# Softmax attention with keys on partitions in two mixers of a four-layer network

## The chip, the cores and the metric

The program runs on one core of one Trainium2 chip, as one launch. Its time is device microseconds for that core. Five engines work side by side, each through an instruction queue of its own: TensorE (PE) multiplies, VectorE (DVE), ScalarE (ACT) and GpSimd (POOL) do elementwise work, SyncE (SP) starts DMAs. Matrix products land in PSUM, everything else is in SBUF.

## The reference

One sequence of 512 tokens with 1024 features passes two blocks. The first has two layers of forgetting attention and sparse attention. The second, where the change lies, has an even layer and an odd layer, each a mixer followed by layer norm, an expert layer and another layer norm. The two attentions in question attend in both directions, in fp32:

```python
# even layer: MLA, 8 heads, 64 + 32 features for the scores (32 rotary key features shared by all heads)
s = (jnp.einsum('bqhd,bkhd->bhqk', qn, k_nope) + jnp.einsum('bqhd,bkd->bhqk', qp, k_pe)) * scale
pr = jax.nn.softmax(s.astype(jnp.float32), axis=-1).astype(v.dtype)
return jnp.einsum('bhqk,bkhd->bqhd', pr, v)
...
# odd layer: 16 query heads of 64 in 4 groups that share keys and values, RMS norm and rotary on q and k
sc = jnp.einsum('bqkgd,bskd->bkgqs', qb, k) * scale
pr = jax.nn.softmax(sc.astype(jnp.float32), axis=-1).astype(v.dtype)
return jnp.einsum('bkgqs,bskd->bqkgd', pr, v)
```

## The kernel before

All activations stay in SBUF with features on partitions and the 512 tokens along the free axis. A product in full precision is made of fp32r passes over exact high and low parts (`h`, `l`): weight parts `whi`, `wlo` by activation parts, three passes for each 128x128 tile of weights (`mm3`). The split of the weights is a cast on ACT and a subtraction on DVE or POOL (L220). Products written as fp32 without a split (`o`, `ss`, `rt`) are recorded as two passes each.

Both mixers handle heads in pairs: four pairs in MLA (`even_mixer`, L1029), eight in the odd mixer (L1703). For one pair `full_pair` (L988) puts 128 queries on partitions. For each half of the queries and each head it makes two score tiles `s` with all 512 keys along the free axis (L1001: three passes in MLA, two in the odd mixer); DVE finds each row's maximum (L1002); ACT takes the exponential with the maximum as bias and adds up the row (L1003); DVE scales the rows by the reciprocal of the sum (L1004, L280). The probabilities are then transposed on PE in 128x128 tiles (`pt`, L1015, sixteen for each half and head), copied to SBUF by DVE (L1021) or ACT (L1019), and multiplied with the values: L1026 writes 64 partitions of `o` for each head, 256 queries at a time, over four tiles of keys. `put_split` (L492) leaves the parts of `o` for the output projection: a cast on ACT (L493) and a subtraction on DVE (L494).

In MLA a pair's queries `qn` and keys `kn` are projected in the loop and scaled into the tiles Q and K, which hold 64 own features and 32 rotary ones of each head; the rest of the query tile is zeroed once by POOL memsets (L1123). In the odd mixer `normed_rope` projects the 128 features of a pair (`qk`), takes their mean squares (`ss`), ACT forms the reciprocal root (L262, L263), the rotation goes through PE (`rt`, L1740) and the two halves of the rotary product are made by DVE (L1742) and POOL (L1743). Keys of a half of the groups come first and again at the fourth pair. The value projection `tm` (L520 to L522) follows the first query projection.

Two pieces of other work fall into the odd mixer's start. The layer norm before it hands over the activations tile by tile: ACT copies the transposed tile, DVE makes its parts (cast L1396, subtraction L1397). POOL multiplies the token-major copy `xtok` by a gain and adds a bias (L1789, L1790), four tiles of 128x1024 each.

The order on each engine is not that of the text. A scheduler moves instructions at build time by its own timing of the dependences, with the order of the text as its start; the pools of tiles (`bufs`) bound how far work can run ahead. The queues then run in that order.

Of the kernel before, what the change touches and what calls it, by code (L numbers as in the profile page):

```python
# [10 lines left out]
F32 = mybir.dt.float32  # L11
# [20 lines left out]
def constants():  # L32
# [10 lines left out]
    # partial rotary: the first 16 of 64 features, pairs (i, i + 8)  # L43
# [21 lines left out]
    # axial rotary  # L65
# [22 lines left out]
    c["before"] = before  # L88
    c["slot"] = np.tile(np.arange(64, dtype=f32)[None, :], (128, 1))
# [3 lines left out]
def layout(inputs):  # L93
    """The arrays as the device takes them: values moved, none computed."""
# [10 lines left out]
    # blocks of 512 rows and columns, and of 256 columns, by partition  # L105
# [20 lines left out]
class Parts(list):  # L126
    """hi and lo of 1024 features, a tile for each 128; a tile can serve as float32 scratch before."""
# [17 lines left out]
class K:  # L145
# [5 lines left out]
    def open(self, es):  # L151
# [10 lines left out]
        # gains of the first block's norms: mix 0, mix 1, mlp 0, mlp 1, final  # L162
# [42 lines left out]
    def split(self, view, pool=False):  # L205
        """Exact two-part split of fp32 weights [128, k, ...]: hi + lo, each float32r [128, k, n]."""
# [16 lines left out]
    def mm3(self, ps, wh, wl, xh, xl, first=True, last=True):  # L223
        """One k-tile of a product, weights stationary: wh*xh + wh*xl + wl*xh."""
# [5 lines left out]
    def proj(self, ps, view, xh, xl, first=True, last=True, pool=False):  # L230
        """ps[m, t] += sum_k view[k, m] x[k, t] over view's k-tiles."""
# [5 lines left out]
    def exp_ln_table(self):  # L237
        """One table of ScalarE that serves Exp and Ln alike."""
# [6 lines left out]
    def add_square(self, pool, ss, x, m):  # L245
        """Sum of squares over eight feature tiles, one at a time."""
# [12 lines left out]
    def rstd_of(self, pool, ss, n, out):  # L259
        """out = (ss / n + eps) ** -0.5"""  # L260
# [11 lines left out]
    def rowvec(self, pool, src, n, name):  # L272
        """[128 * n] of DRAM to [128, n], feature k*128 + p at [p, k]."""
# [64 lines left out]
    def block1(self, xT, A, B):  # L338
        """Both layers of the first block; the final norm's input parts are left in A."""
# [21 lines left out]
    def mixer1(self, l, A, B, mp, mixed, xT, cp):  # L361
        """The two attentions' outputs, hi/lo, into B from the normed input's parts in A."""
# [3 lines left out]
        with ExitStack() as es:  # L366
# [11 lines left out]
            # rstd by token  # L378
# [43 lines left out]
            # running sums of log sigmoid, in two float32r parts: rows 0-7 hi, rows 32-39 lo  # L422
# [20 lines left out]
    def fox(self, l, at, pp, w, XH, XL, v, cneg, B, comp):  # L443
# [19 lines left out]
        def attend(pr):  # L463
# [32 lines left out]
    def log1p_exp_neg(self, p, a, name):  # L496
        """log(1 + exp(-a)) for a >= 0, exact where exp(-a) is small."""
# [11 lines left out]
    def token_major(self, pp, src, XH, XL, outs, rT, tag="mm"):  # L509
        """outs[t][tok, 256] = rstd * (x @ src) with tokens on partitions."""  # L510
# [16 lines left out]
    def token_wide(self, pp, src, XH, XL, outs, rT, first):  # L527
        """outs[t][tok, 512] = rstd * (x @ src) with tokens on partitions."""
# [20 lines left out]
    def rope_in(self, at, rc, rs, z):  # L549
        """z <- z * C + swap(z) * S, the swap within groups of 32 partitions."""  # L550
# [9 lines left out]
    def q_stack(self, at, pp, wv, XH, XL, rope):  # L560
        """Two heads' queries, scaled by 1/8, as [hi; lo] (first) and [lo; hi] (second)."""
# [22 lines left out]
    def causal_scores(self, at, pp, Q, KH, qh, kl, extra=None):  # L584
        """exp(s - max) of a head, four query tiles; and their sums [128, 4]."""
# [22 lines left out]
    def causal_pv(self, at, pp, o, P, cf, V, first, last):  # L608
        """o[64h.., q] += sum_k V[h][k]^T (cf * P)^T for two heads."""
# [22 lines left out]
    def nsa(self, l, p, at, pp, w, XH, XL, gate, gcmp, B, KC, VC, fill):  # L632
# [17 lines left out]
        # vs | vw, tokens on partitions  # L650
# [14 lines left out]
        for g in range(2):  # L665
# [5 lines left out]
            # compressed branch of the four heads  # L671
# [63 lines left out]
    def compress(self, l, p, at, pp, w, XH, XL, B, mixed):  # L735
        """Compressed keys (float32r hi, lo on both halves) and values (four copies of 32 rows)."""
# [3 lines left out]
        # the first product's weights, four rows of [2, 128, 256] each  # L740
# [27 lines left out]
        for kv in range(2):  # L768
# [65 lines left out]
    def merge_fox(self, l, mp, at, pp, w, XH, XL, B, mixed, th):  # L834
        """mixed = the first branch's output by its gate, doubled."""
# [29 lines left out]
    def merge1(self, l, xs, A, B, mixed, ready):  # L865
        """mixed = sigmoid(gates) * branch outputs; x += mixed @ w_out; the mlp's input parts into B."""
# [44 lines left out]
    def new_x(self, p, ss, xs, m, g, B):  # L911
        """Feature tile m is final: its squares into ss, its scaled parts into B."""
# [6 lines left out]
    def mlp1(self, l, xs, A, B):  # L919
        """x += relu(h @ w_up) ** 2 @ w_down; the next layer's input parts into B."""  # L920
# [43 lines left out]
    # ================= block 2 =================  # L964
# [115 lines left out]
    def mla(self, XH, XL, B, pp, lr, sg, silu):  # L1080
# [3 lines left out]
        with ExitStack() as es:  # L1084
# [5 lines left out]
            with ExitStack() as e2:  # L1090
# [33 lines left out]
                for _ in range(2):  # L1124
                    next(silu)
# [686 lines left out]
```

## Time and profile before

| | |
|---|---|
| median of 3 runs | 3559.79 us (3554.05 to 3563.22) |
| profiled execution, span | 3556.4 us |
| PE busy | 3368.4 us, 95% |
| DVE, ACT, POOL busy | 1612.2, 1057.3, 499.1 us |
| share of PE in the chain that ended last | 87% |
| MLA's attention | about 1832 to 1922 us in the span |
| odd mixer with the first part of its output projection | about 2680 to 2912 us |

A row of the timeline gives start, duration and what the instruction waited for; "x8" joins eight in a row. Durations of matmuls overlap, since they are pipelined: the time from one start to the next tells what one costs. In the windows "PEclk" is the granted clock of PE, 1.00 for 2.4 GHz and 0.50 for 1.2 GHz; a value between is a mean over the stretch.

### The profile page before, as it was taken

How to read it: one execution, taken by the hardware profiler on the slowest of the kernel's cores; microseconds unless marked ns; L12 is line 12 of the kernel's file. 1: busy time of each engine (PE TensorE's matmuls, PEld its weight loads, DVE VectorE, ACT ScalarE, POOL GpSimd, SP SyncE). 2: the span in 40 equal slices, each digit the busy share in tenths (PEclk: the TensorE clock that was granted, in tenths of full speed). 3: DMA queues.
4: the chain of work that ended last, by engine and by line, in shares of the span. 5: the costliest groups of instructions: out<-in, count | busy, mean ns of one | idle time of the engine just before them, and what ended most of it. 6: DMA issues, size and time to landing. Idle time of an engine off the chain costs nothing.

```text
span 3556.4 us, 37806 instructions
## 1 busy us (share of the span) xinstructions
PE 3368.4 (95%) x15178; PEld 2159.7 (61%) x15178; DVE 1612.2 (45%) x2560; ACT 1057.3 (30%) x1897; POOL 499.1 (14%) x326
## 2 busy tenths in 40 slices
PE   8999999999999999999989879999998997999997
PEld 6666578887766657888766653444435665344443
DVE  6555464335554546344566651312226764221223
ACT  4333332223333333232364311111114541111111
POOL 2012120002001202001121430000004113000001
PEclk9999999999999999999999889999998998999999
DMA  5111132233211113332220339789881024988986
GB/s 180 48 46 50 31 101 95 95 114 115 68 51 36 48 36 100 99 98 95 66 76 13 121 131 419 322 361 381 353 349 61 24 97 197 402 344 357 384 341 273
DMA packets 219647, 584.85 MB, mean 164 GB/s; under 512 B 17232, under 2 KB 156880, under 8 KB 168272
## 3 DMA queue, kind: packets, MB, share of 16 engines
q1 hardware_dynamic: 219040, 581.66, 43.8%
q8 instruction: 119, 1.95, 0.2%
q10 hardware_dynamic: 432, 0.79, 0.1%
q14 instruction: 56, 0.46, 0.0%
HBM read 580.30 MB, written 2.10 MB: 164 GB/s over the span
## 4 chain that ended last, share of the span: by engine, by line
PE 87%; DVE 7%; ACT 2%; DMA 1%; issue 1%; POOL 0%; SPq 0%; DVEq 0%; ACTq 0%; POOLq 0%
PE a L1611 13%; PE mm L226 8%; PE mm L228 8%; PE mm L227 8%; PE y L1611 7%; PE o L629 3%; PE ga L1622 2%; PE pt L620 2%; PE o L1026 2%; PE s L597 2%; PE mg L226 1%; PE mg L228 1%; PE mg L227 1%; PE s L1001 1%; DMA w<-in_w_dram 1%; PE pt L1015 1%
## 5 line engine op out<-in xcount | busy, mean ns | idle before, releaser
L217 ACT CAST whi<-w 128x1024 fp32r<-128x1024 f32 (+1 forms) x312 | 311.3, 1003 | 740.5 <-PE mm L227 504.6
L1611 PE MATMUL a<-w,xg 128*64 128x512 f32 x2048 | 503.5, 600 | 7.5 <-DMA w<-in_w_dram 7.5
L226 PE MATMUL mm<-h,whi 128*128 128x512 f32 x1056 | 417.7, 396 | 4.9 <-ACT whi L217 4.2
L227 PE MATMUL mm<-l,whi 128*128 128x512 f32 x1056 | 414.2, 393 | 0.0
L228 PE MATMUL mm<-h,wlo 128*128 128x512 f32 x1056 | 413.7, 393 | 0.4 <-POOL wlo L220 0.3
L220 DVE TENSOR_TENSOR wlo<-w,whi 128x1024 fp32r<-128x1024 f32 (+1 forms) x240 | 308.3, 1288 | 225.1 <-ACT whi L217 224.4
L1611 PEld LDWEIGHTS a<-w,xg 128*64 128x64 f32 x2048 | 156.2, 137 | 288.0 <-issue 269.6
L220 POOL TENSOR_TENSOR wlo<-w,whi 128x1024 fp32r<-128x1024 f32 x72 | 158.6, 2205 | 832.3 <-ACT whi L217 740.7
L1611 PE MATMUL y<-w,hT 128*64 128x512 f32 x1024 | 253.7, 598 | 0.2 <-DMA w<-in_w_dram 0.2
L226 PEld LDWEIGHTS mm<-h,whi 128*128 128x128 f32 x1056 | 198.7, 188 | 50.7 <-ACT whi L217 5.4
L228 PEld LDWEIGHTS mm<-h,wlo 128*128 128x128 f32 x1056 | 198.5, 188 | 47.5 <-DVE wlo L220 1.0
L227 PEld LDWEIGHTS mm<-l,whi 128*128 128x128 f32 x1056 | 198.7, 188 | 43.5 <-issue 0.7
L601 DVE TENSOR_REDUCE mx<-s 128x1 f32<-128x128 f32 x192 | 93.3, 489 | 192.3 <-PE s L600 191.3
L1695 DVE TENSOR_TENSOR xtok<-xtok,sc 128x512 f32<-128x512 f32 x128 | 83.8, 683 | 180.6 <-PE sc L1693 180.6
L1611 PEld LDWEIGHTS y<-w,hT 128*64 128x64 f32 x1024 | 75.5, 136 | 132.9 <-issue 125.1
L603 ACT ACTIVATE P<-s,mx 128x128 f32<-128x128 f32 x192 | 100.9, 527 | 175.4 <-DVE mx L601 163.2
L947 POOL TENSOR_TENSOR u<-u 128x512 f32<-128x512 f32 x64 | 66.5, 1040 | 521.6 <-ACT E L946 275.5
L1668 POOL TENSOR_TENSOR og<-OH,aff 128x512 f32<-128x512 f32 x16 | 16.8, 1048 | 723.6 <-PE ot L1671 696.1
L958 DVE TENSOR_TENSOR y<-mm,r 128x512 f32<-128x512 f32 x64 | 44.2, 691 | 160.6 <-PE mm L228 160.6
L1660 DVE SCALAR_TENSOR_TENSOR th<-th,a 128x512 f32<-128x512 f32 x32 | 22.0, 686 | 198.5 <-ACT th L1659 198.5
L226 PE MATMUL mm<-E,whi 128*128 128x512 f32 x256 | 99.6, 389 | 0.0
L228 PE MATMUL mm<-E,wlo 128*128 128x512 f32 x256 | 99.6, 389 | 0.0
(589 smaller groups left out, 6278.3 us busy)
## 6 DMA issues: line engine op xcount, KB each, us to landing
w<-in_w_dram SPq DMA_DIRECT2D x384, 1024.0 KB, 9.9
w<-in_w_in_dram SPq DMA_DIRECT2D x32, 1024.0 KB, 5.3
w<-in_w_up_dram SPq DMA_DIRECT2D x32, 1024.0 KB, 5.4
w<-in_w_down_dram SPq DMA_DIRECT2D x32, 1024.0 KB, 5.0
w<-in_w_out_dram SPq DMA_DIRECT2D x8, 1024.0 KB, 5.0
w<-in_w_o_dram SPq DMA_DIRECT2D x8, 1024.0 KB, 4.8
w<-in_ple_gate_w_dram SPq DMA_DIRECT2D x8, 1024.0 KB, 6.4
w<-in_w_in_even_dram SPq DMA_DIRECT2D x7, 1024.0 KB, 5.5
```

Source lines behind the costliest of these rows:

```text
L217: nc.scalar.copy(h, view)
L220: e.tensor_sub(l, view, h)
L226: mm(ps, wh, xh, start=first, stop=False)
L227: mm(ps, wh, xl, start=False, stop=False)
L228: mm(ps, wl, xh, start=False, stop=last)
L597: nc.tensor.matmul(s[:, :n], qh[:, qs], kl[:, :n], start=False, stop=False)
L601: nc.vector.tensor_reduce(mx[:, i:i + 1], s[:, :n], axis=X, op=OP.max, negate=True)
L603: nc.scalar.activation(pv, s[:, :n], AF.Exp, bias=mx[:, i:i + 1], accum_out=sums[:, i:i + 1])
L620: nc.tensor.transpose(ps[:, (i - k) * 128:(i - k + 1) * 128], P[h][0][i][:, k * 128:(k + 1) * 128], C["ident"])
L629: nc.tensor.matmul(o[64 * h:64 * h + 64, 128 * k:], V[h][k], PT[h][:, :n], start=first and k == 0, stop=last and k == 3)
L1611: nc.tensor.matmul(ps[64 * a:64 * a + 64], lhs(a, 4 * kc + k), cw[a][:, k], start=kc == 0 and k == 0, stop=kc == 1 and k == 3)
L1695: nc.vector.tensor_add(xs, xs, ps)
```

## The change

`full_pair` goes. In its place the scores are made with keys on partitions, so that their exponentials need no transposing before the product with the values.

The maximum of each query's row is found from a cheaper product first (`max_steps`): for each head four single passes of the high parts alone give `s` with queries on partitions, DVE reduces each of them into one column of a tile `mt`, one transposition on PE turns the columns into rows, and DVE spreads the negated maxima over four rows of the query tile, block by block with the constant `diag4`. The key tiles hold ones in these four rows, so the score product itself subtracts the maximum (to the precision of that product, which softmax cancels).

`attend_steps` then makes the score tiles `st` (128 keys by 512 queries, L1023), takes their exponentials without bias or sums (L1025, six tiles `PT`), adds up three of four tiles for the sums (`acc`, L1030: two additions on POOL, one on DVE), multiplies them with the values, 512 queries at a time (L1036), and sums over the partitions by a product with ones (`sm`, L1041). Ln and Exp on ACT give the reciprocal, DVE multiplies, `put_split` follows.

Steps are now lists of small functions, and `weave` calls the steps of several lists by their place in the interval given to each: in MLA the pair j with the maxima of pair j+1; in the odd mixer the pair j, the maxima of j+1 and the projection of j+2, with the second keys at the second pair.

With that go: tiles with rows of zeros and ones (memsets on POOL, in MLA four for each of two key parts and their ones, in the odd mixer sixteen of 64 or 128 partitions at its start and eight small ones), a second query tile per head in the odd mixer (cast on POOL), all of its weight splits on POOL (every fourth to every one before), three PSUM buffers less one for `mm` and one more for `o`, a load of the ACT table for Exp and Ln ahead of MLA's attention, and the gain and bias of `xtok` in pieces of 512 columns, eight and eight.

```diff
+    def weave(self, *lists):
+        at = sorted((a + (b - a) * (i + 0.5) / len(s), n, i)
+                    for n, (s, a, b) in enumerate(lists) for i in range(len(s)))
+        for _, n, i in at:
+            lists[n][0][i]()
+
+    def max_steps(self, pp, q, k, mt, r0, dst):
...
+        def one(i):
+            s = pp.tile([128, T], F32, name="s", tag="s")
+            nc.tensor.matmul(s, q[:, 128 * i:128 * i + 128], k, start=True, stop=True)
+            nc.vector.tensor_reduce(mt[:, r0 + i:r0 + i + 1], s, axis=X, op=OP.max, negate=True)
+
+        def spread():
+            ps = pp.tile([128, 128], F32, name="mt", tag="mm")
+            nc.tensor.transpose(ps, mt, C["ident"])
+            rows = slice(r0, r0 + 4)
+            nc.vector.tensor_tensor(dst[rows]..., ps[rows, None, :]..., C["diag4"][rows]..., op=OP.mult)
+        return [lambda i=i: one(i) for i in range(4)] + [spread]
+
+    def attend_steps(self, at, pp, passes, V, B, j):
...
+        def score(h, k):
+            s = pp.tile([128, T], F32, name="st", tag="t")
+            for n, (kk, qq) in enumerate(passes[h]):
+                nc.tensor.matmul(s, kk[:, 128 * k:128 * k + 128], qq, start=n == 0, stop=n == len(passes[h]) - 1)
+            pt = PT[h, k] = at.tile([128, T], F32, name="PT", bufs=6)
+            nc.scalar.activation(pt, s, AF.Exp)
+            if k == 0:
+                acc[h] = at.tile([128, T], F32, name="acc")
+            else:
+                e = nc.vector if k == 3 else nc.gpsimd
+                e.tensor_add(acc[h], PT[h, 0] if k == 1 else acc[h], pt)
+
+        def values(k):
+            if k == 0:
+                o.append(pp.tile([128, T], F32, name="o", tag="o"))
+            for h in range(2):
+                nc.tensor.matmul(o[0][64 * h:64 * h + 64], V[h][k], PT[h, k], start=k == 0, stop=k == 3)
+
+        def norm():
+            sm = pp.tile([128, T], F32, name="sm", tag="o")
+            for h in range(2):
+                nc.tensor.matmul(sm[64 * h:64 * h + 64], C["ones"][:, :64], acc[h], start=True, stop=True)
+            r = at.tile([128, T], F32, name="rn", tag="PT", bufs=6)
+            nc.scalar.activation(r, sm, AF.Ln)
+            nc.scalar.activation(r, r, AF.Exp, scale=-1.0)
+            nc.vector.tensor_mul(r, r, o[0])
+            self.put_split(B, j, r)
+        sc = [lambda h=h, k=k: score(h, k) for k in range(4) for h in range(2)]
+        va = [lambda k=k: values(k) for k in range(4)]
+        return sc[:6] + va[:1] + sc[6:7] + va[1:2] + sc[7:] + va[2:] + [norm]
...
@@ even_mixer: the loop over pairs
+            tail(0)
+            for j in range(4):
+                V = ...
+                steps = self.attend_steps(at, pp, passes[j], V, B, j)
+                if j < 3:
+                    prepare(j + 1)
+                self.weave((steps, 0, 1), (tops[j + 1] if j < 3 else [], 0.1, 0.8))
...
@@ odd_mixer: keys, queries and the loop over pairs
+                for h in range(2):
+                    r0 = 64 - 64 * h
+                    nc.gpsimd.memset(kl[h][r0:r0 + 64].bitcast(F32), 0.0)
+                    nc.gpsimd.memset(kl[h][r0:r0 + 4].bitcast(F32), 1.0)
+                    nc.vector.tensor_sub(kl[h][64 * h:64 * h + 64], z[own], kh[own])
...
+                    nc.gpsimd.tensor_copy(q2[own], z[own])
+                    steps += self.max_steps(pp, q, kh, mt[j % 2][h], oth.start, q2)
+                    passes[j].append([(kh, q), (kl[h], q2)])
...
+            for j in range(8):
+                g = j // 2
+                V = [[v[:, k, 64 * g:64 * g + 64] for k in range(4)]] * 2
+                lists = [(self.attend_steps(at, pp, passes[j], V, B, j), 0, 1)]
+                if j < 7:
+                    lists.append((queries(j + 1), 0.1, 0.7))
+                if j < 6:
+                    lists.append((project(j + 2), 0.05, 0.45 if j == 1 else 0.6))
+                if j == 1:
+                    lists.append((keys(1), 0.45, 1))
+                self.weave(*lists)
+                s = slice(512 * (j % 2), 512 * (j % 2) + 512)
+                xt = self.xtok[:, j // 2, s]
+                nc.gpsimd.tensor_mul(xt, xt, G[:, s])
+                nc.gpsimd.tensor_add(xt, xt, Bb[:, s])
-                if j < 4:
-                    xt = self.xtok[:, j]
-                    nc.gpsimd.tensor_mul(xt, xt, G)
-                    nc.gpsimd.tensor_add(xt, xt, Bb)
```

In the orders below, `s` and `st` are score tiles before and after with their operands, `pt` transposed probabilities, `o` value products, `sm` sums, `ss` and `rt` the mean squares and the rotation of a projection, `qk` a projection. "x8" joins equal rows.

PE in MLA, in the midst of the second pair, before:

```order
L1001 MATMUL s<-K01h,l_2530 128x512
L1015 MATMUL pt<-c_ident,P 128x128 x8
L1001 MATMUL s<-K01h,h_2528 128x512
L1001 MATMUL s<-K01l,h_2528 128x512
L1001 MATMUL s<-K01h,l_2530 128x512
L1026 MATMUL o<-PT,vm 64x256 x3
L1015 MATMUL pt<-c_ident,P 128x128 x4
L1026 MATMUL o<-PT,vm 64x256
```

And after, at the like place (L1002 is the maximum product for the pair behind):

```order
L1023 MATMUL st<-h_2528,K01h 128x512
L1036 MATMUL o<-PT,vm 64x512
L1023 MATMUL st<-l_2529,K00h 128x512
L1023 MATMUL st<-h_2527,K00l 128x512
L1023 MATMUL st<-h_2527,K00h 128x512
L1036 MATMUL o<-PT,vm 64x512
L1002 MATMUL s<-K10h,h_3401 128x512 x2
L1023 MATMUL st<-l_2530,K01h 128x512
```

The transpositions are gone; the value products, in groups of one to four before, stand singly with three score passes between them, and the next pair's maximum products lie in the gaps.

PE in the odd mixer, in the midst of a pair before:

```order
L1026 MATMUL o<-PT,vo 64x256 x3
L1015 MATMUL pt<-c_ident,P 128x128 x4
L1026 MATMUL o<-PT,vo 64x256
L1001 MATMUL s<-kh_18437,Q_18878 128x512
L1001 MATMUL s<-kl_18438,Q_18878 128x512
L1015 MATMUL pt<-c_ident,P 128x128 x4
L227 MATMUL qk<-l_17521,whi 128x512
L228 MATMUL qk<-h_17513,wlo 128x512
```

And after, at the end of a pair, where its sums product stands:

```order
L1023 MATMUL st<-Q_17831,kh_17565 128x512
L1792 MATMUL ss<-sq,c_ones_17494 128x512
L1023 MATMUL st<-Q_17518,kl_17566 128x512
L1002 MATMUL s<-kh_17565,Q_17831 128x512
L1041 MATMUL sm<-acc,ones 64x512 x2
L1798 MATMUL rt<-z,c_rot 128x512
L1007 MATMUL mt<-c_ident,mt_17501 128x128
L1023 MATMUL st<-Q_17827,kh_17565 128x512
L1023 MATMUL st<-Q_17518,kl_17566 128x512
L1036 MATMUL o<-PT,vo 64x512
```

Where the projection of the pair and its scores alternated with transpositions, the sums product, the rotation, a transposition of maxima and the first scores of the next pair now follow each other.

POOL at the start of the odd mixer, before:

```order
L1668 TENSOR_TENSOR og<-OH,aff 128x512
L220 TENSOR_TENSOR wlo<-w,whi 128x1024
L1789 TENSOR_TENSOR xtok<-xtok,lng 128x1024 x4
L1790 TENSOR_TENSOR xtok<-xtok,lnb 128x1024 x4
L1743 TENSOR_TENSOR z<-z,c_gc 128x512 x2
L220 TENSOR_TENSOR wlo<-w,whi 128x1024 x2
```

And after:

```order
L222 TENSOR_TENSOR wlo<-w,whi 128x1024 x2
L1881 TENSOR_TENSOR xtok<-xtok,lng 128x512 x4
L1882 TENSOR_TENSOR xtok<-xtok,lnb 128x512
L1881 TENSOR_TENSOR xtok<-xtok,lng 128x512 x4
L1882 TENSOR_TENSOR xtok<-xtok,lnb 128x512 x3
L1762 MEMSET mt_17498 128x128
L1762 MEMSET mt_17499 128x128
L1762 MEMSET mt_17500 128x128
L1762 MEMSET mt_17501 128x128
L1809 MEMSET Q_17516 64x512
L1809 MEMSET Q_17517 64x512
```

Eight long pieces on `xtok` become sixteen short ones, with memsets of the new tiles among them, in front of the first rotary product.

## Rows read from the trace of the kernel before

**Rows 1.** The page: span, and each engine's busy time.
```profile
span 3556.4 us, 37806 instructions
...
PE 3368.4 (95%) x15178; PEld 2159.7 (61%) x15178; DVE 1612.2 (45%) x2560; ACT 1057.3 (30%) x1897; POOL 499.1 (14%) x326
```

**Rows 2.** Windows of MLA's attention and the odd mixer, and their sum.
```profile
core 0: us, PE busy (x) PEld busy (x) DVE busy (x) ACT busy (x) POOL busy (x), PEclk, DMA share, GB/s
1832.00:1922.00 90.00, 86.51 (x438) 55.86 (x439) 66.01 (x126) 50.83 (x109) 5.67 (x4) 1.00 0.02 3
2680.00:2720.00 40.00, 30.15 (x129) 22.10 (x128) 24.15 (x19) 11.88 (x18) 21.92 (x9) 0.79 0.11 30
...
2860.00:2900.00 40.00, 34.76 (x173) 19.89 (x172) 33.95 (x62) 23.34 (x55) 7.61 (x5) 0.91 0.25 83
...
sum 322.00, PE 300.09 PEld 194.81 DVE 226.90 ACT 169.91 POOL 64.70; mean PE 60.02 PEld 38.96 DVE 45.38 ACT 33.98 POOL 12.94
```

**Rows 3.** PE timeline in MLA (start us, us, engine, line, operation, count, wait).
```profile
1858.65 1.03 PE L1015 MATMUL pt<-c_ident,P 128*128 128x128 f32 x8
1859.44 0.48 PE L1001 MATMUL s<-K11h,h 128*128 128x512 f32 x1
...
1861.82 1.08 PE L1026 MATMUL o<-PT,vm 128*64 128x256 f32 x8
...
1865.71 0.39 PE L1001 MATMUL s<-K11h,l 128*128 128x512 f32 x1
1866.03 0.65 PE L1026 MATMUL o<-PT,vm 128*64 128x256 f32 x2
1866.61 1.09 PE L1015 MATMUL pt<-c_ident,P 128*128 128x128 f32 x8
```

**Rows 4.** PE timeline around a value product with 512 columns in another mixer.
```profile
107.99 1.07 PE L629 MATMUL o<-PT,va 128*64 128x512 f32 x2
108.99 0.50 PE L227 MATMUL kp<-l,whi 128*128 128x512 f32 x1
109.33 0.40 PE L228 MATMUL kp<-h,wlo 128*128 128x512 f32 x1
109.57 0.39 PE L226 MATMUL kp<-h,whi 128*128 128x512 f32 x1
```

**Rows 5.** Groups of the whole span (count | busy us, mean ns | idle before).
```profile
L1015 PE MATMUL pt<-c_ident,P 128*128 128x128 f32 x384 | 60.7, 284 | 1.5 <-DVE P L280 1.3
...
L1026 PE MATMUL o<-PT,vo 128*64 128x256 f32 x256 | 51.0, 411 | 2.7 <-DVE l L494 2.4 <-ACT PT L1019 0.2
...
L1026 PE MATMUL o<-PT,vm 128*64 128x256 f32 x128 | 25.9, 397 | 0.8 <-ACT PT L1019 0.7
```

**Rows 6.** PE's waits: odd mixer, then MLA (us in total, times, longest).
```profile
PE s L1001 <- ACT P L1003: 3.2, 4, 1.3
...
PE s L1001 <- ACT P L1003: 1.5, 3, 0.9
```

**Rows 7.** DVE and POOL timelines at the odd mixer's start.
```profile
2679.61 0.69 DVE L1397 TENSOR_TENSOR l<-xf,h 128x512 fp32r<-128x512 f32 x1
...
2682.84 2.75 DVE L1397 TENSOR_TENSOR l<-xf,h 128x512 fp32r<-128x512 f32 x1
...
2693.39 2.72 DVE L1397 TENSOR_TENSOR l<-xf,h 128x512 fp32r<-128x512 f32 x1
...
2679.68 10.63 POOL L1789 TENSOR_TENSOR xtok<-xtok,lng 128x1024 f32<-128x1024 f32 x4 [5.94 <-PE xt L1393]
```

**Rows 8.** Groups of POOL (the third of 2715 to 2908 alone) and ACT.
```profile
L947 POOL TENSOR_TENSOR u<-u 128x512 f32<-128x512 f32 x64 | 66.5, 1040 | 521.6 <-ACT E L946 275.5 <-ACT h L946 246.0
...
L1123 POOL MEMSET l<- 32x512 f32 x4 | 2.1, 520 | 38.8 <-PE mm L227 38.6
...
L220 POOL TENSOR_TENSOR wlo<-w,whi 128x1024 fp32r<-128x1024 f32 x8 | 19.0, 2374 | 58.0 <-ACT whi L217 58.0
...
L1072 ACT ACT_TABLE_LOAD x2 | 2.6, 1283 | 0.0
```

More of the change, by code (lines that the diff above doesn't have):

```diff
@@ L1088, in mla @@
             v = p.tile([128, 4, 512], F32, name="vm")
+            mt = [p.tile([128, 128], F32, name=f"mt{b}") for b in range(2)]
+            for m in mt:
+                nc.gpsimd.memset(m, 0.0)
+            self.const(p, "diag4")
             cq, ckv, zpe = [], None, []
@@ L1161, in mla, with prepare @@
             at = es.enter_context(self.pool("mlat", 2))
-            for j in range(4):
+            B.renew(1, 2, 3)
+            self.exp_ln_table()
+            passes, tops = {}, {}
+            def prepare(j):
                 a = j % 2
@@ L1710, in odd_mixer @@
             pp = es.enter_context(self.pool("odp", 2, PSUM))
-            gc, gs, rot, o64 = [self.const(p, n) for n in ("gc", "gs", "rot", "ones64")]
+            gc, gs, rot, o64, _ = [self.const(p, n) for n in ("gc", "gs", "rot", "ones64", "diag4")]
+            mt = [[p.tile([128, 128], F32, name=f"mt{a}{b}") for b in range(2)] for a in range(2)]
+            for m in mt[0] + mt[1]:
+                nc.gpsimd.memset(m, 0.0)
             gq = p.tile([128, 1], F32, name="gq")
@@ L1747, in odd_mixer @@
             KS = []
+            Q2 = [[p.tile([128, T], F32R, name=f"Q2{a}{h}") for h in range(2)] for a in range(2)]
+            for a in range(2):
+                for h in range(2):
+                    nc.gpsimd.memset(Q2[a][h][64 - 64 * h:128 - 64 * h].bitcast(F32), 0.0)
             self.exp_ln_table()
             def keys(j):
[L1751 to L1760 removed]
@@ L1762, in odd_mixer @@
-            keys(0)
-            for j in range(8):
-                if j == 2:
-                    self.every = 1
-                if j == 3:
-                    keys(1)
-                if j % 2 == 0:
-                    raw = self.wcols(w, 128 * j)
-                z = normed_rope(raw[:, :, (j % 2) * 128:(j % 2) * 128 + 128], gq)
-                if j == 0:
-                    self.token_major(pp, w[:, 1280:1536], XH, XL, [v[:, t] for t in range(4)], one, "t")
+                z = []
+                steps = normed_rope((lambda: self.wcols(w, 1024 + 128 * j, 128)) if j else (lambda: k0), gk, z)
@@ new lines, in keys, with key_parts @@
+                return steps + [lambda b=b: key_parts(j, b, z[0]) for b in range(2)]
+            def key_parts(j, b, z):
+                own = slice(64 * b, 64 * b + 64)
+                kh = p.tile([128, T], F32R, name=f"kh{2 * j + b}")
+                kl = [p.tile([128, T], F32R, name=f"kl{2 * j + b}{h}") for h in range(2)]
+                for o_ in (slice(0, 64), slice(64, 128)):
+                    nc.scalar.copy(kh[o_], z[own])
+                for h in range(2):
[3 more added lines that the diff above has]
+                    nc.vector.tensor_sub(kl[h][64 * h:64 * h + 64], z[own], kh[own])
+                KS.append((kh, kl))
@@ L1773, in odd_mixer, with weights, project, queries @@
+            raws, zq, passes = {}, {}, {}
+            def weights(j):
+                if j % 2 == 0:
+                    raws[0] = self.wcols(w, 128 * j)
+                return raws[0][:, :, (j % 2) * 128:(j % 2) * 128 + 128]
+            def project(j):
+                zq[j] = []
+                return normed_rope(lambda: weights(j), gq, zq[j])
+            def queries(j):
+                z = zq.pop(j)[0]
                 kh, kl = KS[j // 2]
-                passes = []
+                passes[j], steps = [], []
@@ L1778, in odd_mixer, with run @@
                     q = at.tile([128, T], F32R, name=f"Q{h}")
+                    q2 = Q2[j % 2][h]
                     nc.scalar.copy(q[own], z[own])
                     nc.vector.tensor_sub(q[oth], z[own], q[own])
-                    passes.append([(q, kh), (q, kl)])
+                    nc.gpsimd.tensor_copy(q2[own], z[own])
+                    steps += self.max_steps(pp, q, kh, mt[j % 2][h], oth.start, q2)
+                    passes[j].append([(kh, q), (kl[h], q2)])
+                return steps
+            def run(steps):
+                for s in steps:
+                    s()
+            run(keys(0))
+            run(project(0))
+            self.token_major(pp, w[:, 1280:1536], XH, XL, [v[:, t] for t in range(4)], one, "t")
+            tops = queries(0)
+            self.weave((tops, 0, 1), (project(1), 0, 1))
+            for j in range(8):
                 g = j // 2
                 V = [[v[:, k, 64 * g:64 * g + 64] for k in range(4)]] * 2
-                o = pp.tile([128, T], F32, name="o", tag="o", bufs=1)
-                self.full_pair(at, pp, o, passes, V)
-                self.put_split(B, j, o)
-                if j < 4:
-                    xt = self.xtok[:, j]
-                    nc.gpsimd.tensor_mul(xt, xt, G)
-                    nc.gpsimd.tensor_add(xt, xt, Bb)
+                lists = [(self.attend_steps(at, pp, passes[j], V, B, j), 0, 1)]
[10 more added lines that the diff above has]
+                nc.gpsimd.tensor_add(xt, xt, Bb[:, s])
 _OUTS = [((1, 512, 1024), "float32")]
```

107 lines of the change are left out of this document (39 added, 68 removed).

## Prediction, made before the changed kernel was run

> **What bounds the kernel now.** I read the page first: TensorE (PE) is busy for 95% of a span of 3556.4 us [rows 1], so it is the engine to count. Then the windows over the two stretches that the change touches: the attention of the MLA heads (1832 to 1922 us) and the odd mixer (2680 to 2912). PE is busy for 300.09 of their 322.00 us while DVE works 226.90, ACT 169.91 and POOL 64.70 [rows 2]. So at most 21.9 us of waits lie there, plus what the clock costs where it was granted at a mean of 0.79 or 0.91 [rows 2]. All the rest is PE's own work: a change here pays by what it takes from PE's work or from these waits. Then the PE timeline, from start to next start, for the price of each kind of matmul, and the waits and the other engines' timelines for the start of the odd mixer.
>
> The profiled execution spans 3556.4 us, 3.4 below the median of the three runs (3559.79), inside their spread of 9.2; I count from the span and leave the difference alone.
>
> **PE work, by pieces.** Score products keep their number (three 512-column passes per 128 queries in MLA, two in the odd mixer, now per 128 keys).
>
> *Transposes go.* 384 of 128x128. Eight of them reach from 1858.65 to 1859.44, 0.10 each [rows 3]; the busy time of the line is 60.7 us [rows 5], 0.16 each, which counts overlap with neighbours. I take 0.11: -42 us (ends -38 and -61).
>
> *Maximum products come.* 8 per pair of heads, 96 in all, fp32r with 512 columns, 0.24 from start to start as between 109.33 and 109.57 [rows 4], 0.23 as the rule in long rows of them: +22. Transposing the 24 sets of maxima: 24 x 0.11 = +3.
>
> *Value products and sums.* These write 64 partitions, in fp32. A trace records two passes for one such matmul ("x2"). One with 256 columns that stands alone goes from 1866.03 to 1866.61, 0.58, and the matmul ahead of it takes 0.32 instead of 0.23 (1865.71 to 1866.03) [rows 3]. One with 512 columns takes 1.00 (107.99 to 108.99) and slows the next to 0.34 [rows 4]. Four in a row, heads alternating, take 1.08 with 256 columns [rows 3]: five passes of some 0.216 and not eight, so the second pass of one head runs beside the first of the other. I therefore count a group of n adjacent matmuls as n + 1 passes, of 0.216 (256 columns, 1.08 / 5) or 0.427 (512, about twice that), plus edges of 0.30 (entry, last pass, next matmul; 0.36 for 512 columns). Before: 192 matmuls in 80 groups by the order: 272 x 0.216 + 80 x 0.30 = 83 us (busy time of the line: 51.0 + 25.9 = 76.9 [rows 5]). After: 96 value products and 24 for the sums, all 512 columns. In the new order score products stand between the two heads' value products nearly everywhere, so these 120 matmuls form 103 groups, 91 of them of one: 223 x 0.427 + 103 x 0.36 = 132 us. Difference +49. With no edges at all after it would be 95 - 77 = +18; with every matmul alone, 120 x 1.21 (1.00 + 0.10 + 0.11) - 77 = +68.
>
> PE work in sum: -42 + 22 + 3 + 49 = **+32 us** (ends -18 and +55). The transposes' saving is eaten by the rows of ones for the sums and by heads that no longer share passes.
>
> Here the Trainium skill ("TensorE: Matmul & The Clock Gate", Part 3: Packing small matmuls) says that matmuls on different column groups run concurrently when each one's output goes to its own partitions. The rows agree only by half, five passes where the rule would give four for four matmuls. By the rule the old groups would have been cheaper still and the new, isolated products worth as much as here, so that the step would cost more than +49; the sum above does not use it.
>
> **Waits that go.** (a) Start of the odd mixer. DVE prepares the split of x (a cast and a subtraction for each tile) while POOL multiplies and adds the token copy in 128x1024 pieces, four in 10.63 us [rows 7]. In this stretch the subtraction takes 2.75 us, against 0.69 just before [rows 7]: each DVE instruction ends with a POOL instruction. PE waits for them: from 2680 to 2720 it is busy for 30.15 of 40 us, at a mean clock of 0.79 [rows 2], so part of this time at the lower of its two levels. The change halves these POOL pieces to 512 columns, so that a pair of DVE instructions should cost some 2.7 us instead of 5.3. Five DVE instructions at this pace fill the time from 2682.84 to 2696.11 [rows 7]; at half of it, PE's chain ends 6 to 7.5 us earlier, and about 3 us of half clock behind it go: -10.5 in all (0 if the pieces slow DVE as long as before; at most the 9.9 us idle and the clock's 0.21 x 30.15 = 6.3 [rows 2], -16). The Trainium skill ("SBUF — State Buffer", Who interferes with whom) says that a DVE instruction with two SBUF inputs and a GpSimd instruction that reads SBUF exclude each other, while one that only writes does not. The rows agree for the subtraction; whether the new memsets leave DVE alone no row here shows.
>
> (b) End of the odd mixer, 2860 to 2900: idle 5.2 us and the clock at 0.91, 0.09 x 34.76 = 3.1 [rows 2]; with the next pair's products woven in, I take -8. (c) Elsewhere PE's waits for the exponential, 3.2 us in the odd mixer and 1.5 in MLA [rows 6], belong to the old chain score, maximum, exponential, scale, transpose: -4.
>
> Together **-23** (ends -5 and -31, where -31 is all 21.9 us idle and 9.4 of clock: 6.3 + 3.1).
>
> **Waits that come.** At the end of each pair the chain is now sums product, Ln, Exp, multiply, split; and the PSUM tile of the next scores is freed by an exponential. The nearest rows are those seven waits for the exponential, 4.7 us in all, 0.67 each [rows 6]. Eleven pair ends at that price: +7 (ends 0 and, two such waits at each, +15). Behind the last pair nothing is woven, and the chain has three instructions more, 0.69 each by the DVE row [rows 7]: +2 (0 to 2). POOL gets memsets of 0.52 us [rows 8] at the start of the odd mixer, 16 before the last halves of the token copy, 8.3 us in its queue, ahead of the rotary multiplication for the first keys. PE has the value projection and two query projections to do there, so most is covered: +2.5 (0 to 8). Three more ACT table loads of 1.28 us [rows 8], in front of the exponentials: +1 (0 to 4). POOL's running sums, 24 x 2 additions of 1.04 us [rows 8] beside the 22 us that each of four MLA pairs takes, and the DVE reductions, whose number stays, are hidden by PE's work; what it costs when this cover goes is the third rival. Sum **+12** (0 to 29).
>
> Net: 32 - 23 + 12 = +21, so 3556.4 + 21 = 3577 us.
>
> **Rivals.**
> 1. *Nothing measurable.* The edges are no cost of the matmul itself but lie in gaps that the new neighbours fill: then before counts 272 x 0.216 = 59, after 95, +36 in place of +49, and the net is +8: 3564. For: the rows with edges all come from mixed neighbourhoods. Against: the 0.32 and 0.34 repeat whatever stands beside them. Chance 0.22.
> 2. *Faster.* As 1, and the weaving takes away all 31 us of waits and brings no new ones: 32 - 13 - 31 = -12, 3544. For: PE's waits here are all on ACT and DVE chains [rows 6], and these get a whole pair of slack. Against: waits at the start of the odd mixer have nothing woven in front of them. Chance 0.14.
> 3. *Much slower: POOL's queue.* The tiles of exponentials have 6 buffers for the 8 of a pair, and two of each head's four are freed by POOL's additions. If such an addition stands behind a weight split (2.37 us) and a rotary product (1.04, as the addition, for its size) [rows 8], the next exponential has no buffer, the score tile stays full, and PE stops for up to 3.4 us. Once in each of seven odd pairs: +24, 3601. It decides as soon as POOL is late by more than two exponentials' worth of PE work, about 2 us. For: POOL's instructions slow down when DVE reads beside them. Against: POOL is busy for only a fifth of these stretches now [rows 2]. Chance 0.19.
> 4. The scheduler undoes the weaving: the order after shows the next pair's maximum products between this pair's scores, so this has 0.02.
>
> **How the numbers follow.** Forecast 0.43, rivals 0.22, 0.14, 0.19, 0.02. A change under 0.3% (10.7 us) can't be told from none. The forecast's own range, PE work from +20 to +45, is 3565 to 3590, a tenth of it within 0.3%; with rivals 2 and 3 cut at their far sides: 3550 to 3603. Faster 0.15, same 0.25, slower 0.60.
>
> **What would show it.** In the changed profile: value products of 1.0 us start to start with 0.3 edges, and a busy sum near 132 us for value products and sums (near 95: rival 1); the windows of both stretches with PE at 98% and at full clock; DVE's subtractions at the start of the odd mixer at some 1.4 us (2.7: term (a) wrong); no PE wait behind a POOL addition (rival 3). A shorter odd mixer with isolated value products would refute the pass count, the largest term.

## The result, and the profile after

The changed kernel takes 3600.9 us (median of four runs, 3595.85 to 3605.05) against 3561.5 before, a ratio of 1.0113 (95% interval 1.0094 to 1.0131): slower by some 40 us. The direction was forecast, the size was not: 3577 stands 24 us under it. Some 5 of these 24 us are the base: the forecast counted from a span of 3556.4 us, and the median before is 3561.5. The time lies at the upper end of the range, 3550 to 3603.

The profiled execution spans 46.4 us more than that of before. Of these 4.2 are there already when MLA's first query projection starts (1836.2 us in the span, 1832.0 before), and they arise ahead of MLA, in code that did not change; the two executions differ there in the granted clock (0.97 against 0.99 in the first 400 us). The medians differ by 39.4.

The page after, to be held against [rows 1]:

```profile
span 3602.8 us, 36933 instructions
...
PE 3409.3 (95%) x14770; PEld 2139.3 (59%) x14770; DVE 1576.9 (44%) x2426; ACT 1033.3 (29%) x1779; POOL 602.6 (17%) x442
```

PE works 41 us more and keeps its share of 95%. Next, three windows of each kernel, with the same beginnings and ends in the program: MLA from its first `qn` to the first product behind it (`gz`); the odd mixer from the first transpose of x to the last pass of the first keys; and from there to the output projection. The columns are those of [rows 2]; first before, then after.

```profile
1832.00:1922.50 90.50, 87.01 (x440) 55.99 (x440) 66.01 (x126) 50.83 (x109) 5.67 (x4) 1.00 0.01 3
2667.90:2696.80 28.90, 17.77 (x56) 12.24 (x56) 26.62 (x24) 9.89 (x15) 19.74 (x8) 0.62 0.14 46
2696.80:2908.50 211.70, 200.55 (x995) 129.66 (x993) 144.10 (x260) 115.52 (x239) 42.22 (x23) 0.97 0.15 51
sum 331.10, PE 305.33 PEld 197.90 DVE 236.74 ACT 176.23 POOL 67.64; mean PE 101.78 PEld 65.97 DVE 78.91 ACT 58.74 POOL 22.55
```

```profile
1836.20:1942.40 106.20, 98.96 (x305) 47.17 (x305) 58.14 (x85) 44.43 (x72) 29.46 (x29) 0.94 0.04 10
2684.60:2713.50 28.90, 16.72 (x56) 11.83 (x56) 26.27 (x22) 10.00 (x15) 25.84 (x21) 0.55 0.15 45
2713.50:2954.40 240.90, 222.08 (x723) 109.50 (x721) 121.33 (x170) 95.83 (x157) 108.52 (x92) 0.98 0.13 42
sum 376.00, PE 337.75 PEld 168.50 DVE 205.75 ACT 150.26 POOL 163.82; mean PE 112.58 PEld 56.16 DVE 68.58 ACT 50.09 POOL 54.61
```

PE's busy time grows from 305.33 to 337.75 us, by 32.4, and its idle time from 25.8 to 38.3, by 12.5; that is 44.9 us, of which the expert layer between the two mixers gives 3.2 back. The middle stretch, in which 7 us and more were to be won, has kept its 28.9 us to the tenth. The value and sums products after, in groups as in [rows 5]:

```profile
L1036 PE MATMUL o<-PT,vo 128*64 128x512 f32 x128 | 66.3, 617 | 0.0
...
L1036 PE MATMUL o<-PT,vm 128*64 128x512 f32 x64 | 29.9, 632 | 0.0
...
L1041 PE MATMUL sm<-acc,ones 128*64 128x512 f32 x48 | 20.9, 613 | 0.7 <-DVE acc L1030 0.7
```

117.1 us in place of 76.9. On the timeline of PE in MLA's last pair (start, duration, as in [rows 3]) one sees what one costs alone and what two cost side by side:

```profile
1932.66 0.40 PE L1023 MATMUL st<-h,K10h 128*128 128x512 f32 x1
1932.98 1.07 PE L1036 MATMUL o<-PT,vm 128*64 128x512 f32 x2
1933.99 0.50 PE L1023 MATMUL st<-l,K11h 128*128 128x512 f32 x1
1934.32 0.39 PE L1023 MATMUL st<-h,K11l 128*128 128x512 f32 x1
1934.55 0.40 PE L1023 MATMUL st<-h,K11h 128*128 128x512 f32 x1
1934.88 1.08 PE L1036 MATMUL o<-PT,vm 128*64 128x512 f32 x4
1935.89 0.66 PE L1262 MATMUL rt<-c_ident,rB 128*128 128x128 f32 x4
```

Alone (1932.98) 1.01 us to the next start, and that next one takes 0.33. The four records at 1934.88 are the two heads' products side by side: also 1.01 us, so the second costs nothing. At the odd mixer's start DVE and POOL do this (to be held against [rows 7]):

```profile
2697.33 1.63 DVE L1445 TENSOR_TENSOR l<-xf,h 128x512 fp32r<-128x512 f32 x1
2698.89 1.48 DVE L1444 CAST h<-xf 128x512 fp32r<-128x512 f32 x1
2700.40 0.69 DVE L1445 TENSOR_TENSOR l<-xf,h 128x512 fp32r<-128x512 f32 x1
2701.01 1.49 DVE L1444 CAST h<-xf 128x512 fp32r<-128x512 f32 x1
...
2692.22 6.20 POOL L1881 TENSOR_TENSOR xtok<-xtok,lng 128x512 f32<-128x512 f32 x4
```

With halved pieces a held-up DVE instruction takes about half as long, 1.5 to 1.65 us in place of 2.6 to 2.75. But POOL now begins at 2692.22, while the transposes still run (until 2701); before, it began with the last of them.

PE's waits in the odd mixer from 2690 us on, as in [rows 6]:

```profile
PE xt L1441 <- ACT xf L1443: 6.8, 3, 2.8
PE st L1023 <- ACT PT L1025: 5.7, 6, 1.2
PE qk L228 <- ACT xf L1443: 4.1, 1, 4.1
PE rt L1798 <- DVE z L1796: 3.5, 4, 1.2
PE qk L228 <- DVE zs L1800: 2.0, 3, 0.7
PE tm L522 <- ACT whi L219: 1.9, 2, 1.0
PE ss L1792 <- DMA c_ones<-in_const_dram: 1.9, 1, 1.9
```

### The profile page after: what moved, and what is told of

Read it like the earlier page. It is cut to its first block, busy times and chain, and to the rows that moved or that the text cites. A ratio compares the mean times of both kernels' runs of the same rounds, so it can differ in the third digit from the quotient of the medians.

```text
span 3602.8 us, 36933 instructions
## 1 busy us (share of the span) xinstructions
PE 3409.3 (95%) x14770; PEld 2139.3 (59%) x14770; DVE 1576.9 (44%) x2426; ACT 1033.3 (29%) x1779; POOL 602.6 (17%) x442
## 4 chain that ended last, share of the span: by engine, by line
PE 88%; DVE 6%; ACT 2%; DMA 2%; issue 1%; POOL 1%; SPq 0%; DVEq 0%; ACTq 0%; POOLq 0%
PE a L1659 13%; PE mm L230 8%; PE mm L228 8%; PE mm L229 8%; PE y L1659 7%; PE o L631 3%; PE o L1036 2%; PE ga L1670 2%; PE pt L622 2%; PE s L599 2%; PE st L1023 2%; PE mg L228 1%; PE mg L230 1%; PE mg L229 1%; DMA w<-in_w_dram 1%
```

## The experiments

Ratios are to the kernel before, with 95% intervals.

**MLA alone.** The kernel before with the new `mla` and its helpers; the odd mixer's code is the old one.

> Before, with the new MLA attention alone; the odd mixer stays the old one. Work theory (PE's own work carries the loss: isolated value products, sums products): MLA's stretch, from the first query projection to the first product behind it, grows from 90.6 us to about 106, as in the changed kernel, of which some 11 us are PE work and 4 a wait; the expert layer behind it, which waits for weights, gives some 7 us back; in all +8 to +12 us. Rival (waits from the weaving of both mixers): the stretch grows by under 5 us of PE work and the rest is waits of over 10 us.

1.0024 (1.0014 to 1.0035), +8.6 us. MLA's window:

```profile
1830.90:1937.10 106.20, 98.94 (x304) 47.19 (x304) 58.16 (x85) 44.41 (x72) 29.44 (x29) 0.94 0.04 10
```

The stretch is 106.2 us, as in the changed kernel. PE is busy for 98.94 us of it (87.01 before) and idle for 7.3 (3.5): by busy time the work theory holds, and the rival's order of the two falls. But some 6 of the 12 us of busy time are clock (a mean of 0.94 in place of 1.00), which neither counted: at full clock the work grew by about 6. Not all of the 15.7 us arrives at the end: the expert layer behind MLA and the odd mixer, whose order the scheduler set anew although its code is the old one, are 3 and 6 us shorter.

**The odd mixer alone.** The kernel before with the new `odd_mixer` and its helpers.

> Before, with the new odd mixer alone; MLA stays the old one. Work theory: from the first key product to the output projection 227.4 us grow to about 249, PE's gaps in it stay near 17 to 19 us, and the transposes of x ahead of it lose another 6 to 8 us to DVE; +28 to +31 us in all. Rival (the loss in the odd mixer comes from what MLA left behind, or from the clock): under +20 us.

1.0083 (1.0069 to 1.0097), +29.6 us, as the work theory has it.

```profile
2703.90:2944.50 240.60, 221.78 (x723) 109.37 (x721) 121.77 (x171) 95.75 (x157) 108.48 (x92) 0.98 0.13 43
```

The stretch from the first keys to the output projection is 240.6 us (211.7 before), PE idle for 18.8 us of it (11.2 before). With MLA alone this makes 38, about the 40 of both.

**The halves of the token copy in the kernel before.**

```diff
-                if j < 4:
-                    xt = self.xtok[:, j]
-                    nc.gpsimd.tensor_mul(xt, xt, G)
-                    nc.gpsimd.tensor_add(xt, xt, Bb)
+                s = slice(512 * (j % 2), 512 * (j % 2) + 512)
+                xt = self.xtok[:, j // 2, s]
+                nc.gpsimd.tensor_mul(xt, xt, G[:, s])
+                nc.gpsimd.tensor_add(xt, xt, Bb[:, s])
```

> Before, with the gain and bias of the token copy in pieces of 512 columns and nothing else changed. The prediction's term (a): DVE's casts and subtractions at the odd mixer's start cost half, the chain of the first keys ends 6 to 7.5 us earlier, -7 to -10 us in all. Rival (halves start earlier, as soon as the first half of the transposes has read its columns, and so slow DVE's instructions for all eight tiles and not for the last four): the casts and subtractions cost some 1.5 us each but twice as many of them do, PE waits for the transposes' evictions as well, and the first keys end where they did: -2 to +3 us.

1.0015 (1.0006 to 1.0024), +5.3 us: the term of the prediction is refuted, the rival a little exceeded. POOL's timeline of this kernel, whose first transpose of x starts at 2674.9:

```profile
2680.71 6.71 POOL L1789 TENSOR_TENSOR xtok<-xtok,lng 128x512 f32<-128x512 f32 x4
2687.38 4.79 POOL L1790 TENSOR_TENSOR xtok<-xtok,lnb 128x512 f32<-128x512 f32 x3
2692.54 3.15 POOL L1789 TENSOR_TENSOR xtok<-xtok,lng 128x512 f32<-128x512 f32 x2 [0.38 <-PE xt L1393]
```

POOL's first piece starts 5.8 us behind the first transpose; before it was 11.8 us (2667.9, where the second window of before begins, and 2679.68 in [rows 7]). A piece of 512 columns needs only the first four transposes to have read it, a piece of 1024 all eight. The short pieces hold up nearly all of DVE's splitting (its eight subtractions take 1.55 us on the mean); PE waits 8.3 us between transposes for the activation, which in turn waits 15.0 us for subtractions that free its buffer, and the keys end 31.0 us after the first transpose, not 28.9.

**The token copy held back, in the kernel before.** The gain gets a harmless rewrite that needs the last tile, and POOL keeps the order of the text.

```diff
             nc.vector.memset(one, 1.0)
+            nc.vector.scalar_tensor_tensor(G[:, :1], XL[7][:, :1].bitcast(F32), 0.0, G[:, :1], op0=OP.mult, op1=OP.add)
...
-                    nc.gpsimd.tensor_mul(xt, xt, G)
-                    nc.gpsimd.tensor_add(xt, xt, Bb)
+                    self.tc.keep_in_program_order(nc.gpsimd.tensor_mul(xt, xt, G))
+                    self.tc.keep_in_program_order(nc.gpsimd.tensor_add(xt, xt, Bb))
```

> Before, with the gain and bias of the token copy held back until DVE has split the last tile of x (the gain's first column is rewritten, unchanged, from that tile), and then in the order of the text on POOL. If POOL's instructions are what slows DVE there: DVE's casts at 0.4 and subtractions at 0.7 us throughout, the first keys' product ends 5 to 8 us earlier, and -4 to -8 us in all, less what the long POOL pieces then cost between the pairs. Rival (the low clock and the activation ahead of each tile bind, not POOL): under 2 us gained.

0.9998 (0.9989 to 1.0007): no gain that can be told. By the time alone this is what the rival forecast; the two windows of the odd mixer decide:

```profile
2672.40:2693.70 21.30, 16.45 (x56) 12.21 (x56) 14.28 (x26) 9.88 (x15) 2.63 (x1) 0.56 0.28 80
2693.70:2909.20 215.50, 199.02 (x995) 128.82 (x993) 160.43 (x259) 115.27 (x239) 58.80 (x29) 0.98 0.14 48
```

The first part is 7.6 us shorter, with DVE's casts at 0.42 and subtractions at 0.69 us throughout: POOL is what held up DVE, and the rival falls. But the second part is 3.8 us longer, DVE works 160 us in it and not 144: the held pieces now fall between the pairs and hold DVE there. A hold-up that is moved is paid elsewhere, in these two windows half of it; a gain of the other half, 3.8 us, would lie at the edge of the interval.

**The two heads' products side by side**, in the changed kernel.

```diff
-                nc.tensor.matmul(o[0][64 * h:64 * h + 64], V[h][k], PT[h, k], start=k == 0, stop=k == 3)
+                self.tc.keep_in_program_order(nc.tensor.matmul(o[0][64 * h:64 * h + 64], V[h][k], PT[h, k], start=k == 0, stop=k == 3))
...
-                nc.tensor.matmul(sm[64 * h:64 * h + 64], C["ones"][:, :64], acc[h], start=True, stop=True)
+                self.tc.keep_in_program_order(nc.tensor.matmul(sm[64 * h:64 * h + 64], C["ones"][:, :64], acc[h], start=True, stop=True))
```

> The changed kernel, with the two heads' value products and sums products kept in the order of the text on PE, so that nearly all of them stand side by side. Pairing theory (two heads' products run fully beside each other: in the changed kernel's trace two adjacent ones of 512 columns take 1.009 us, one alone 1.003): the 97 groups of value and sums products become about 53, each saved one worth 1.0 us and 0.2 of edges, less what groups of three to six cost; 118 us of them become about 77, so -35 to -42 us against the changed kernel, about even with the kernel before. Prediction's count (n + 1 passes): a pair costs 1.5 singles, so -15 to -20. Rival (the time lost sits in waits, and PE work saved turns into longer waits for exponentials and POOL's sums): under -12.

1.0035 (1.0024 to 1.0045): +12.0 us to the kernel before, 27 less than the changed kernel's 39, where 35 to 42 were expected. The eleven executions range from 3565 to 3582 us; the profiled one, 3567.8, is among the fastest, so its windows show rather more than the 27. The groups and windows:

```profile
L1036 PE MATMUL o<-PT,vo 128*64 128x512 f32 x128 | 38.5, 611 | 0.0
...
L1036 PE MATMUL o<-PT,vm 128*64 128x512 f32 x64 | 20.5, 716 | 0.0
...
L1041 PE MATMUL sm<-acc,ones 128*64 128x512 f32 x48 | 15.8, 625 | 0.0
```

```profile
1827.00:1926.80 99.80, 86.73 (x305) 47.77 (x305) 58.97 (x85) 43.78 (x72) 29.75 (x29) 0.90 0.04 10
2673.30:2702.10 28.80, 16.15 (x56) 11.23 (x56) 26.15 (x22) 9.99 (x15) 25.74 (x20) 0.59 0.14 46
2702.10:2917.50 215.40, 194.54 (x723) 107.82 (x721) 127.42 (x171) 94.49 (x157) 106.28 (x92) 0.97 0.15 49
sum 344.00, PE 297.42 PEld 166.83 DVE 212.54 ACT 148.26 POOL 161.77; mean PE 99.14 PEld 55.61 DVE 70.85 ACT 49.42 POOL 53.92
```

The products cost 74.8 us in place of 117.1, as the pairing theory has it (42 less; n + 1 passes would have saved half of it). PE is busy for 40 us less in the three windows. Of these 8 turn into waits: idle goes from 38.3 to 46.6 us, and MLA's clock from 0.94 to 0.90. So the rival has a part of it, a fifth. MLA shows it best: PE is busy for 86.73 us there (87.01 before the change), and yet the stretch is 9 us longer, for PE waits 5.3 us for the transposition of the maxima, which hangs on DVE's reductions, and 4.2 us for a weight behind the last pair.

**The same, with the token copy held back.**

> As the one before (paired products), and the gain and bias of the token copy held until the last tile of x is split, then in the order of the text on POOL. If POOL's lock on DVE's port is what the odd mixer's start loses: the transposes of x and the first keys go 8 to 12 us faster than in the changed kernel, of which 4 to 8 are left at the end; -40 to -50 us against the changed kernel, and so 3 to 10 us faster than the kernel before. Rival (the held POOL work delays rotary products and sums between the pairs): no gain over the paired kernel.

1.0003 (0.9995 to 1.0012): even with the kernel before, so some 12 us gained over the paired kernel and the rival refuted, though 3 to 10 us under the kernel before were expected. The two edits together take back the whole loss. From the first transpose to the output projection it takes 235.5 us (240.6 before); MLA's 99.6 (90.5 before) take it back.

**Without the sums products.**

```diff
-            sm = pp.tile([128, T], F32, name="sm", tag="o")
-            for h in range(2):
-                nc.tensor.matmul(sm[64 * h:64 * h + 64], C["ones"][:, :64], acc[h], start=True, stop=True)
-            nc.scalar.activation(r, sm, AF.Ln)
+            nc.scalar.activation(r, acc[0], AF.Ln, bias=C["eps"])
```

> The changed kernel without the sums products: the reciprocal is taken from the running sums of one head in their place, so the division by the right sums is left out. Work theory: 24 products of 64 columns in 19 groups go, 19 x 1.2 = 23 us, and part of PE's 9 us of waits in front of them: -23 to -30 us. Rival (they stand in gaps that PE would wait out anyway): under -10.

1.0082 (1.0066 to 1.0098): some 11 us less than the changed kernel, with intervals that touch, where 23 to 30 were expected: a miss. In the three windows PE is busy for 322.09 us, 15.7 less, and idle for 44.5, 6.3 more. At the ends of the pairs little else is ready: what PE no longer does there it partly waits out, for exponentials (6.7 us in the odd mixer, 5.7 with the sums) and for the rotary chain.

**The token copy held back in the changed kernel.**

> The changed kernel with the gain and bias of the token copy held until the last tile of x is split, then in the order of the text on POOL; nothing else. From the first transpose of x to the end of the first keys 28.9 us become about 21, as in the kernel before with the same hold; at the end -4 to -10 us against the changed kernel. Rival (the memsets in front of it and POOL's sums take the place): under -3.

1.0087 (1.0072 to 1.0101): 7 to 9 us less than the changed kernel, as expected, though the intervals overlap. The first part of the odd mixer takes 21.9 us in place of 28.9.

**All running sums on DVE.**

```diff
-                e = nc.vector if k == 3 else nc.gpsimd
+                e = nc.vector
```

> The changed kernel with all running sums of exponentials on DVE, none on POOL. The prediction's third rival (additions late in POOL's queue hold the buffers of exponentials): 10 us or more faster. Theory (in the changed kernel's trace ACT waits for such an addition once, 1.1 us, so POOL's queue holds nobody): within 4 us of the changed kernel, to the slower side if DVE's reductions come later for it.

1.0099 (1.0083 to 1.0114), within the runs of the changed kernel. POOL's additions hold nobody; the prediction's third rival falls.

**The old MLA, and the new odd mixer with both edits.**

> The old MLA, and the new odd mixer with paired value and sums products and the token copy held back. In the kernel with both new mixers and these two edits, MLA's stretch was 9 us longer than before and the odd mixer, from the first transpose of x to the output projection, 5 us shorter (235.5 against 240.6). If the stretches stand for themselves: 3 to 6 us faster than the kernel before. Rival (what one stage gains the next one waits out): within 2 us of it.

0.9990 (0.9981 to 0.9999): 3559.4 us beside 3563.4, some 3.5 us faster than the kernel before, if by little more than can be told. The windows of it, MLA first:

```profile
1835.10:1925.70 90.60, 87.10 (x441) 56.09 (x441) 66.07 (x126) 50.87 (x109) 5.67 (x4) 1.00 0.02 3
2671.10:2693.30 22.20, 16.10 (x55) 11.64 (x56) 15.65 (x24) 9.99 (x15) 17.97 (x27) 0.57 0.30 89
2693.30:2906.70 213.40, 194.15 (x723) 106.81 (x721) 141.07 (x171) 94.78 (x157) 112.50 (x84) 0.97 0.15 48
```

MLA is as before; the odd mixer takes 235.6 us, 5.0 less. It is the only version here that is faster than both kernels.

## Why the prediction was wrong

*PE work, +32: right in size.* Busy time grew by 32.4 us. Some 5 of it is clock: busy time times one minus the clock is 12.8 us before and 17.9 after, by the windows above. At full clock the work grew by about 27.

*The pass count was wrong within it.* I read four products in 1.08 us, a duration, as five passes. The rows behind it on the same timeline of before give the time from start to start:

```profile
1862.84 0.66 PE L1015 MATMUL pt<-c_ident,P 128*128 128x128 f32 x4
1863.42 1.08 PE L1026 MATMUL o<-PT,vm 128*64 128x256 f32 x6
1864.43 0.50 PE L1001 MATMUL s<-K10h,h 128*128 128x512 f32 x1
```

The four products that start at 1861.82 end with the next start at 1862.84, 1.02 us; the three from 1863.42 to 1864.43 take 1.01. Both are four passes of 0.216 and edges, so two heads overlap fully; after, 1.01 us for one and for two. Here the Trainium skill ("TensorE: Matmul & The Clock Gate", Part 3: Packing small matmuls) was right, which says that products on different column groups run concurrently, and my weighing of it was not. The sum hardly suffered, since for groups of one and of three matmuls n + 1 is the right count: by the traces 91 of the 103 groups after are of one, and of the 80 before 34 are of one and 35 of three. The products' own busy time grew by 40 us, for a term of +49; the busy sum, 117.1, lies between the two signs that I had named, 132 and 95 (rival 1). The difference stands with the neighbours, whose delay the term counts and the products' lines do not: the median pass ahead of a lone product takes 0.33 us and the one behind it 0.34, in place of 0.23.

*Waits that go, -23: this step failed, and with it the forecast.* Taken together the waits did not go. Idle time rose by 12.5 us and the clock cost 5 more, where the step and the one behind it (+12) made -11 together. By its parts:
- (a) Start of the odd mixer, -10.5: nothing. I priced one held-up DVE instruction right (about half) and counted them by the old schedule. Shorter pieces depend on less, start earlier, and hold up twice as many; alone, in the kernel before, they lose 5.3 us.
- (b) and (c) -12: PE's waits for the old chain went, and larger ones came. (b) came true in part: in the last 48.5 us of the stretch idle time fell from 5.4 to 3.9 us and the clock rose from 0.93 to 1.00, together some 4.5 of the 8 us. But from the first keys to the output projection PE is idle for 18.8 us, 11.2 before; in the middle, where little was idle before (3.2 us from 2720 to 2860), it is 10.1 (2740 to 2905.9). The list of waits names the exponential that frees a score tile (5.7 us, six times), the rotary product (3.5), and at the start the value projection's weights and the constant of the mean squares (1.9 each). In MLA stand two that I had not counted:

```profile
PE gz L1326 <- DMA WG<-in_gla_gate_w_bwd_dram: 4.0, 1, 4.0
PE qn L228 <- ACT vm L1191: 3.0, 1, 3.0
```

That is 3.0 us ahead of the first pair, for the last copy of the values (1.6 before; it lies ahead of the window), and 4.0 us behind the last, for a weight whose memset stands on POOL behind five others, the first of which waits for a sums product. This second one is about all that MLA's idle time grew by (3.5 to 7.2 us). PE's clock is at its lower level (0.50) from 1838 to 1840 and from 1845 to 1853 us, after PE had stood still for the 3.0 us and in four waits of 0.3 to 0.8 us between 1840 and 1845; MLA's mean falls from 1.00 to 0.94. That these waits brought the clock down was not tried apart.

*Waits that come, +12:* the pair ends were sized about right (5.7 and 3.5 us against 7), the two stretches' edges were missing. The run without the sums shows that they stand in part where PE waits anyway: 15.7 us of work went, and 6.3 came back as idle time.

*Rivals.* The first (no edges) falls: the passes beside an isolated product still take 0.33 and 0.34 us. The second falls with the waits. The third falls by the run with all sums on DVE. What happened, new waits larger than the old ones beside heavier work, was none of them. Why the waits for exponentials remain with a whole pair's work woven in was not tried apart, nor were the smaller parts of the change (a PSUM buffer less for the projections, other engines for the weight splits).

## What to carry to other kernels

Price a removed wait only when you can name what PE does in that time and what that in turn waits for; weaving changes who is late, and work taken from a place where PE waits is not won in full. Matmuls of 64 output columns belong side by side, one for each half of the output's partitions: emission order alone does not keep them there where a scheduler orders by readiness. And when an instruction is cut in two, look at what each half depends on, since an earlier start may collide with more.

## What the runs showed of the hardware

Two fp32 products of 512 columns into different halves of the partitions take 1.009 us together, and one alone 1.003 (medians of the changed kernel's trace, from start to next start). DVE's casts and subtractions, of one and of two SBUF inputs, both end with a running POOL multiplication: at 0.42 and 0.69 us free, 1.5 and 1.6 beside pieces of 512 columns, 2.6 and 2.75 beside those of 1024. With the token copy held back in the changed kernel, POOL's memsets run beside the splitting:

```profile
2691.26 2.56 POOL L1810 MEMSET Q<- 64x512 f32 x4
2692.15 0.66 DVE L1444 CAST h<-xf 128x512 fp32r<-128x512 f32 x1
2692.84 0.69 DVE L1445 TENSOR_TENSOR l<-xf,h 128x512 fp32r<-128x512 f32 x1
```

The subtractions take 0.69 us there, as when POOL is idle: the memsets leave them alone. So says the Trainium skill ("SBUF — State Buffer", Who interferes with whom) of GpSimd instructions that only write beside a DVE instruction with two SBUF inputs, which the prediction had left open. The casts are not left alone: the six that start beside a memset take 0.66 or 0.67 us, and 0.42 free.
